# Ends of two-stream stages: row-scaled products behind the second root, low weight parts split behind the scaled columns, high-part products first

## The chip, the cores and the metric

One core of one Trainium2 chip runs the whole program in one launch. The metric is the device time of one execution in microseconds (us), as the median of several runs. TensorE (PE) does the matrix products, ScalarE (ACT) and VectorE (DVE) the work on columns and rows, GpSimd (POOL) some additions, SyncE (SP) issues the DMA transfers.

## The reference

A backbone of two layers over 512 tokens of width 1024: 256 context tokens (stream CS, columns 0 to 255 of every tile) and 256 latent tokens (stream XS, columns 256 to 511). Both streams use the same weights and differ in the modulation vectors. In each layer there are three sub-layers: a feed-forward net, a mixer (attention, mLSTM, HGRN2) and a second feed-forward net. All three have the same frame:

```
h = rms_norm(x, g_pre) * (1 + scale) + shift          # ada_pre
y = (silu(h @ w1) * (h @ w3)) @ w2                     # feed-forward; the mixer has its own
x = x + w * gate * rms_norm(y, g_post)                 # ada_post
```

So the end of one sub-layer and the start of the next hold two normalisations over the width in a row. The first needs the mean square of y, the second that of the new x; the new x depends on the first.

## The kernel before, in words

Activations lie transposed: 8 tiles of 128 channels (d = 0 to 7) by 512 tokens. `XT` is the residual x. A weight stage works on units of 512 rows by 256 columns: SP loads the unit as f32 into one of three `raw` buffers, ACT casts it to a high part `wh` (L238), DVE subtracts to get the low part `wl` (L239). There are four `wh` and four `wl` buffers. `h` is split in the same way into a high and a low half. Each product is then three matmuls (`mm3`): high by high (L255), high by low (L256), low by high (L257). A matmul has 256 tokens where the streams run one after the other, 512 where they run together.

**The stage end** (class `Post`). Each of the last output tiles y(d) is copied, squared and multiplied with XT by ACT and DVE, and column sums are taken on PE (L476, L478). They give, per stream, the mean squares of y, of the scaled y, of y times x and of x, and so both normalisations: a first reciprocal root y1 from the sum of y squared, then the mean square of the new x by a short formula, then a second root y2. Both are computed on DVE on 128 by 2 numbers (`rsqrt_cols`, L360 to L369). `steps` is a generator that is advanced from outside: it computes y1; yields; spreads y1 over the partitions on PE (`row_bcast`, L374) into the first half of a PSUM tile (`r`); computes y2; multiplies the eight y tiles by r on DVE (L530) and adds them to XT on POOL (L531); yields; spreads y2 into the second half of the same PSUM tile (`r2`, again L374, so it waits for the eight L530 that read the tile); yields; and forms h from XT and r2 by `scaled` (DVE, L389) and `split` (ACT for the high half, L397; DVE for the low half, L398).

**The stage start** (`passes`). Four accumulators (three PSUM banks `a`, one bank `b`) take a first pass over CS and a second one over XS, 8 channel tiles by 4 accumulators by 3 matmuls, 96 matmuls each. During the CS pass the steps of XS are pending, and `passes` advances them behind channel tiles 0, 2 and 5 and at its end. While the first four units of such a stage are loaded, `part_end` advances the steps of CS. There are four such stages with two streams: the mixers of both layers (mix0, mix1), the second feed-forward net of layer 0 (F1_0) and the first of layer 1 (F0_1). The last feed-forward net (F1_1) has only XS and also goes through `passes`; the very first one goes through its own path with a `hook`.

**What sets the order.** Each engine runs its instructions in the order in which the program holds them. A scheduler of the framework writes that order out when the program is built, from the order of the code, its own estimates of durations and readiness, and extra edges put in by `tc.issue_after(x)` (not before x in time). At a stage's end the units of the following columns (`wh`5 to `wh`8, as counted from the stage's first unit) are in that order too: their casts stand on ACT beside the splits of XS and the first reads of the finished accumulators. Those reads are, in a feed-forward net, silu (L611, one read of each of two accumulators) and in a mixer two activations (L839, L840, both read the same accumulator). PE's next products go to the banks that these reads set free.

Of the kernel before, what the change touches and what calls it, by code (L numbers as in the profile page):

```python
# [74 lines left out]
def body(tc, I, out, dbg=None):  # L75
    nc = tc.nc
    with tc.tile_pool(name="cst", bufs=1) as cst, \
# [9 lines left out]
        def nm(p):  # L87
            cnt[0] += 1
            return f"{p}{cnt[0]}"
# [153 lines left out]
        def unit(src, nk, hold=False, eng=None):  # L243
            res = []
            for b in range(0, nk, 4):
                n = min(4, nk - b)
                res += unit_split(unit_load(src[128 * b:128 * (b + n)], n), hold, eng)
            return res

        def mm3(ps, w, c0, h, a, b, first, last):  # L250
            n = len(w)
# [167 lines left out]
        class Post:  # L419
# [82 lines left out]
            def steps(self, st, pre, rest=None):  # L502


                if rest:
                    after = yield
                    with tc.issue_after(after):
                        rest()
                lo, hi, s = st
                y1 = rsqrt_cols(self.cs[s][:, :, 0], 2, 1.0 / D)  # L510
                t, m = small((128, 2, 4)), small((128, 2))
                V.tensor_scalar(t, self.cs[s], 1.0 / D, None, op0=ALU.mult)
                V.tensor_scalar(t[:, :, 2], t[:, :, 2], 2.0, None, op0=ALU.mult)
                V.tensor_scalar(t[:, :, 3], t[:, :, 3], EPS, None, op0=ALU.add)
                for i, q in ((2, t[:, :, 1]), (3, m)):
                    for k in range(2):
                        V.tensor_scalar(m[:, k:k + 1], q[:, k:k + 1], y1[:, k:k + 1], t[:, k, i:i + 1], op0=ALU.mult, op1=ALU.add)
                V.tensor_scalar(m, m, EPS, None, op0=ALU.max)
                after = yield
                rr = mx()  # L520
                r, r2 = rr[:, 0:256], rr[:, 256:512]
                with tc.issue_after(after) if after is not None else nullcontext():
                    row_bcast(y1, 0, 2, r)
                y2 = rsqrt_cols(None, 2, None, m)
                post_x.clear()
                for d in range(KD):
                    yt = self.y(d)[:, lo:hi]
                    xt = XT[:, d, lo:hi]
                    with tc.issue_after(tail[0]) if st is self.streams[-1] else nullcontext():
                        V.tensor_tensor(yt, yt, r, op=ALU.mult)  # L530
                    post_x.append(G.tensor_tensor(xt, xt, yt, op=ALU.add).ins)  # L531
                after = yield
                with tc.issue_after(after) if after is not None else nullcontext():
                    row_bcast(y2, 0, 2, r2)
                yield
                if pre.A is None:
                    pre.A = pre_cols(pre.l, pre.j, 0, KD)
                for d in range(KD):
                    pre.chunk(d, pre.A[:, d, :], st, r2)
                    if d % 4 == 3:  # L540
                        yield
# [44 lines left out]
        def passes(accs, h, sts, hook=None):  # L586
            settle()
            for p_ in pend[:-1]:
                while p_.left:
                    p_.step()  # L590
            for s_, (lo, hi, _) in enumerate(sts):
                for i in range(KD):
                    for j, (ps, w, c0) in enumerate(accs):
                        if hook:
                            hook(i, j)
                        end = mm3(ps[:, lo:hi], w[i:i + 1], c0, h[i:i + 1], lo, hi, i == 0, i == KD - 1)
                    if s_ == 0 and pend and (i, pend[-1].left) in ((0, 5), (2, 4), (5, 3)):
                        pend[-1].step(end)
                drain(end)

        def ffn(l, f, h, post, streams, pre, first=(None, None)):
# [16 lines left out]
            for gi in range(KF // 2):  # L618
                cols = slice(256 * gi, 256 * gi + 256)
                if gi == 0:  # L620
                    if units:
                        u1, u3 = units
                    else:
                        u1, u3 = [], []
                        for b0 in range(2):
                            with ExitStack() as es:
                                if len(streams) == 1:
                                    for e in (*post_done, *([post_x[2]] if b0 else [])):
                                        es.enter_context(tc.issue_after(e))
                                for u, w, e in ((u1, W1, G if b0 == 0 else V), (u3, W3, G if b0 == 0 else V)):  # L630
                                    u += unit(w[512 * b0:512 * b0 + 512, cols], 4, eng=e if len(streams) == 1 else V)
                            part_end()
                    ps = four()
                    passes([(ps[0], u1, 0), (ps[1], u1, 128), (ps[2], u3, 0), (ps[3], u3, 128)], h,
                           [(a, b, 0)] if hook else streams, hook)
# [188 lines left out]
        def mix(l, h, post, need_c, pre):  # L824
# [20 lines left out]

            us = [[], []]
            for b0 in range(2):
                for u in range(2):
                    us[u] += unit(Win[512 * b0:512 * b0 + 512, OFF_HF + 256 * u:OFF_HF + 256 * u + 256], 4)
                part_end()  # L850
            ps = four()
            passes([(ps[i], us[i // 2], 128 * (i % 2)) for i in range(4)], h, [CS, XS])
            for i in range(4):
# [595 lines left out]
```

## Time and profile before

| | us |
|---|---|
| median of 3 runs | 2438.77 |
| lowest, highest run | 2437.29, 3833.87 |
| the profiled execution | 2436.24 |
| span of its trace | 2434.4 |
| PE busy in the span | 2373.0 |
| ACT busy | 969.1 |
| DVE busy | 1477.4 |

PE is busy in 97% of the span, so the time is close to a sum of matmuls, and what can be won or lost at the same work is PE's idle time (the span less the busy time, 61 us, some of it at the start and the end) and the time in which the throttle granted half the clock. The view of windows gives the granted clock of a stretch as a share of the full one (PEclk); 0.50 is the lower of two levels, 1.2 GHz, and 1.00 the upper one, 2.4 GHz. The mean over the span is 0.985. The view of waits names, for each idle stretch of PE, the instruction that waited and the one that released it. In the timeline a row stands for one or several like instructions, with the start of the first and the time until the last one ended; a matmul of 256 columns is written with 0.28 us, but since matmuls overlap, they follow each other in less.

The stretches of the stages that the change touches, by the span's clock: mix0 405 to 460 us, F1_0 990 to 1065, F0_1 1405 to 1457, mix1 1800 to 1850, F1_1 2200 to 2250.

### The profile page before, as it was taken

To read this page: it belongs to the slowest core of one execution; us is meant where nothing else is said; L and a number is where in the kernel's file an instruction comes from. 1 tells how busy PE (TensorE), PEld (TensorE's weight loads), DVE (VectorE), ACT (ScalarE), POOL (GpSimd) and SP (SyncE) were. 2 spreads that over 40 slices of the span, in tenths; PEclk is the share of its full clock that TensorE was granted. 3 is DMA by queue.
4 is the path that set the end of the run, shared out by engine and by line. 5 is a ranking of instruction groups with operands and counts; after the bars stand their busy time and mean duration, and the time that the engine had idled before them with its cause. 6 is when DMAs were issued, how large, how long until landed. Compare 5 with 4: busy or idle time off the path is not lost.

```text
span 2434.4 us, 34696 instructions
## 1 busy us (share of the span) xinstructions
PE 2373.0 (97%) x13770; PEld 2008.1 (82%) x13770; DVE 1477.4 (61%) x2677; ACT 969.1 (40%) x1591; POOL 240.9 (10%) x233
## 2 busy tenths in 40 slices
PE   8999999999999999999999999999999989998998
PEld 5877878888787788887778888778799889797998
DVE  5687466655644643767946366874546657556554
ACT  3322332434643733432223332232334364754543
POOL 2000022100000112310002120001221000023000
PEclk9999999999999999999999999999999999998999
DMA  8655343311122032345543335653323115253664
GB/s 265 206 193 189 106 149 102 93 36 54 44 70 86 27 100 91 96 139 199 183 138 104 104 98 180 211 178 99 121 83 87 40 57 148 87 156 118 187 186 134
DMA packets 267270, 301.00 MB, mean 124 GB/s; under 512 B 11709, under 2 KB 233206, under 8 KB 267108
## 3 DMA queue, kind: packets, MB, share of 16 engines
q1 hardware_dynamic: 266448, 298.04, 39.2%
q8 instruction: 108, 1.77, 0.3%
q0 software_dynamic: 512, 0.68, 0.2%
q14 instruction: 54, 0.44, 0.1%
q10 hardware_dynamic: 148, 0.06, 0.0%
HBM read 297.70 MB, written 1.05 MB: 123 GB/s over the span
## 4 chain that ended last, share of the span: by engine, by line
PE 90%; DVE 5%; ACT 3%; issue 1%; DMA 1%; POOL 0%; SPq 0%; DVEq 0%; ACTq 0%; POOLq 0%
PE a L255 24%; PE a L256 24%; PE a L257 24%; PE a L767 1%; PE a L768 1%; PE a L769 1%; PE x L883 1%; PE x L320 1%; PE x L374 1%; PE b L1240 1%; PE x L1300 1%; PE x L1273 1%; PE b L256 1%; PE b L257 1%; PE b L255 1%
## 5 line engine op out<-in xcount | busy, mean ns | idle before, releaser
L255 PE MATMUL a<-s,wh 128*128 128x512 f32 (+1 forms) x3266 | 1144.8, 352 | 7.7 <-ACT s L397 7.2
L256 PE MATMUL a<-s,wh 128*128 128x512 f32 (+1 forms) x3266 | 1142.5, 350 | 3.2 <-DVE s L398 2.8
L257 PE MATMUL a<-s,wl 128*128 128x512 f32 (+1 forms) x3266 | 1141.1, 350 | 0.0
L239 DVE TENSOR_TENSOR wl<-raw,wh 128x1024 fp32r<-128x1024 f32 (+1 forms) x414 | 515.9, 1257 | 467.0 <-ACT wh L238 465.0
L255 PEld LDWEIGHTS a<-s,wh 128*128 128x128 f32 x3266 | 618.7, 190 | 110.0 <-ACT wh L238 10.1
L256 PEld LDWEIGHTS a<-s,wh 128*128 128x128 f32 x3266 | 620.5, 190 | 90.4 <-DVE s L398 4.9
L257 PEld LDWEIGHTS a<-s,wl 128*128 128x128 f32 x3266 | 620.1, 190 | 87.6 <-DVE s L615 2.5
L238 ACT CAST wh<-raw 128x1024 fp32r<-128x1024 f32 (+1 forms) x418 | 431.3, 1035 | 607.3 <-PE a L256 427.6
L311 DVE SCALAR_TENSOR_TENSOR s<-s,sc,s 128x512 f32<-128x512 f32 x448 | 306.7, 758 | 0.0
L415 POOL TENSOR_TENSOR s<-s,t 128x512 f32<-128x512 f32 (+1 forms) x35 | 52.4, 1496 | 1019.3 <-ACT s L411 1017.0
L612 DVE TENSOR_TENSOR u<-u,a 128x512 f32<-128x512 f32 (+1 forms) x84 | 51.8, 619 | 101.8 <-PE a L257 99.0
L614 ACT CAST s<-u 128x512 fp32r<-128x512 f32 (+1 forms) x88 | 49.0, 567 | 143.2 <-DVE u L612 125.5
L611 ACT ACTIVATE u<-a 128x512 f32<-128x512 f32 (+1 forms) x88 | 47.5, 542 | 144.8 <-PE a L257 144.8
L397 ACT ACTIVATE s<-t,mod 128x256 fp32r<-128x256 f32 x88 | 38.6, 500 | 93.7 <-DVE t L389 93.7
L767 PE MATMUL a<-wh,s 128*128 128x256 f32 x256 | 73.0, 285 | 2.1 <-ACT s L770 2.1
L768 PE MATMUL a<-wl,s 128*128 128x256 f32 x256 | 73.0, 285 | 0.3 <-DVE wl L239 0.3
L769 PE MATMUL a<-wh,s 128*128 128x256 f32 x256 | 72.8, 284 | 0.0
L531 POOL TENSOR_TENSOR XT<-XT,s 128x256 f32<-128x256 f32 x72 | 56.7, 826 | 132.7 <-DVE s L530 58.3
L1173 POOL TENSOR_TENSOR s<-s,u 128x512 f32<-128x512 f32 (+1 forms) x32 | 35.8, 1121 | 318.6 <-ACT wh L238 172.6
L615 DVE TENSOR_TENSOR s<-u,s 128x512 fp32r<-128x512 f32 (+1 forms) x88 | 53.4, 620 | 15.6 <-ACT s L614 15.2
L461 POOL TENSOR_TENSOR s<-s,u 128x512 f32<-128x512 f32 (+1 forms) x29 | 36.8, 1269 | 209.7 <-DVE u L457 200.4
L446 ACT ACTIVATE s<-a,R 128x256 f32<-128x256 f32 x77 | 34.1, 472 | 53.3 <-PE a L257 46.7
(345 smaller groups left out, 2373.8 us busy)
## 6 DMA issues: line engine op xcount, KB each, us to landing
raw<-in_ffn_w_dram SPq DMA_DIRECT2D x256, 512.0 KB, 3.8
s<-in_w_ada_dram SPq DMA_DIRECT2D x144, 512.0 KB, 6.0
raw<-in_w_in_dram SPq DMA_DIRECT2D x112, 512.0 KB, 3.7
raw<-in_w_out_dram SPq DMA_DIRECT2D x16, 512.0 KB, 3.5
raw<-in_ffn_w_dram SPq DMA_DIRECT2D x16, 256.0 KB, 2.6
raw<-in_w_branch_hg_dram SPq DMA_DIRECT2D x8, 512.0 KB, 4.1
raw<-in_w_branch_ml_dram SPq DMA_DIRECT2D x8, 512.0 KB, 3.3
raw<-in_w_branch_att_dram SPq DMA_DIRECT2D x8, 512.0 KB, 4.6
```

The source lines that it names most:

```text
L238: S.copy(hi[:, :n], raw[:, :n])
L239: (eng or V).tensor_tensor(lo[:, :n], raw[:, :n], hi[:, :n].bitcast(F32), op=ALU.subtract)
L255: mm(ps, hi, h[i][:, 0, a:b], start=first and i == 0, stop=False)
L256: mm(ps, hi, h[i][:, 1, a:b], start=False, stop=False)
L257: end = mm(ps, lo, h[i][:, 0, a:b], start=False, stop=last and i == n - 1)
L311: V.scalar_tensor_tensor(t[:, s], w, c, t[:, s], op0=ALU.mult, op1=ALU.add)
L415: eng.tensor_tensor(dst[:, a:b], dst[:, a:b], q[:, a:b], op=ALU.add)
L531: post_x.append(G.tensor_tensor(xt, xt, yt, op=ALU.add).ins)
L615: V.tensor_tensor(gt[:, 1, a:b], t[:, a:b], gt[:, 0, a:b].bitcast(F32), op=ALU.subtract)
L767: mm(ps, h[k][:, 0, tk], hi, start=k == 0, stop=False)
L768: mm(ps, h[k][:, 0, tk], lo, start=False, stop=False)
L769: mm(ps, h[k][:, 1, tk], hi, start=False, stop=k == KD - 1)
```

## The change

Three edits. (1) In `steps` the eight products y times r (L530) are held back behind the second root for both streams; before, only for the last stream. (2) A function `unit_parts` loads and casts a unit and hands the low subtraction back as a function; in the four two-stream stages the first units are cast at once and their low parts are subtracted after `part_end`, that is behind the scaled columns of CS. (3) `passes` works on blocks of four channel tiles: first all matmuls with the high weight part (both halves of h), then those with the low part. The pending steps of XS are advanced behind tiles 0 and 4 and at the end of the pass, so that y2 is spread only after the CS pass. The path with `hook` keeps its order. Behind line 249 the line numbers of the changed kernel are higher by 9, in `passes` and later by more.

```diff
+        def unit_parts(src, nk):
+            raw = raw_load(src, nk)
+            hi = stg.tile([128, 4, 256], F32R, name=nm("wh"), tag="wh", bufs=NHI)
+            lo = stg.tile([128, 4, 256], F32R, name=nm("wl"), tag="wl", bufs=NHI)
+            S.copy(hi[:, :nk], raw[:, :nk])
+            return [(hi[:, i], lo[:, i]) for i in range(nk)], lambda: V.tensor_tensor(
+                lo[:, :nk], raw[:, :nk], hi[:, :nk].bitcast(F32), op=ALU.subtract)
...
-                    with tc.issue_after(tail[0]) if st is self.streams[-1] else nullcontext():
+                    with tc.issue_after(tail[0]):
                         V.tensor_tensor(yt, yt, r, op=ALU.mult)
...
-                for i in range(KD):
-                    for j, (ps, w, c0) in enumerate(accs):
-                        if hook:
-                            hook(i, j)
-                        end = mm3(ps[:, lo:hi], w[i:i + 1], c0, h[i:i + 1], lo, hi, i == 0, i == KD - 1)
-                    if s_ == 0 and pend and (i, pend[-1].left) in ((0, 5), (2, 4), (5, 3)):
-                        pend[-1].step(end)
+                def one(ps, w, h_, part, i):
+                    for wi, hj in ((0, 0), (0, 1)) if part == 0 else ((1, 0),):
+                        e = mm(ps[:, lo:hi], w, h_[:, hj, lo:hi], start=i == 0 and part == 0 and hj == 0, stop=i == KD - 1 and part == 1)
+                    return e.ins
+                for i0 in range(0, KD, 1 if hook else 4):
+                    blk = range(i0, i0 + (1 if hook else 4))
...
+                    for part in range(2):
+                        for i in blk:
+                            for ps, w, c0 in accs:
+                                end = one(ps, w[i][part][:, c0:c0 + 128], h[i], part, i)
+                            if part == 0 and s_ == 0 and pend and (i, pend[-1].left) in ((0, 5), (4, 4)):
+                                pend[-1].step(end)
                 drain(end)
...
                         for b0 in range(2):
+                            if len(streams) == 2:
+                                los = []
+                                for u, w in ((u1, W1), (u3, W3)):
+                                    w, lo = unit_parts(w[512 * b0:512 * b0 + 512, cols], 4)
+                                    u += w
+                                    los.append(lo)
+                                part_end()
+                                for lo in los:
+                                    lo()
+                                continue
...
             us = [[], []]
             for b0 in range(2):
+                los = []
                 for u in range(2):
-                    us[u] += unit(Win[512 * b0:512 * b0 + 512, OFF_HF + 256 * u:OFF_HF + 256 * u + 256], 4)
+                    w, lo = unit_parts(Win[512 * b0:512 * b0 + 512, OFF_HF + 256 * u:OFF_HF + 256 * u + 256], 4)
+                    us[u] += w
+                    los.append(lo)
                 part_end()
+                for lo in los:
+                    lo()
```

The scheduler writes a new order from this. ScalarE at the end of the XS pass of mix0: before, from the third-last split of h to the reads of the first accumulators (`wh` names with 3763 to 3841 are the four units of the next columns, `a` the accumulators).

```order
L397 ACTIVATE s_3446<-t_3645,mod_88 128x256
L397 ACTIVATE s_3451<-t_3649,mod_88 128x256
L397 ACTIVATE s_3456<-t_3653,mod_88 128x256
L238 CAST wh_3763<-raw_3761 128x1024
L238 CAST wh_3769<-raw_3767 128x1024
L839 ACT_TABLE_LOAD
L839 ACTIVATE s_3376<-a_3459 128x512
L840 ACTIVATE s_3378<-a_3459 128x512
```

And the same place in the changed kernel:

```order
L406 ACTIVATE s_3444<-t_3645,mod_88 128x256
L238 CAST wh_3763<-raw_3761 128x1024
L406 ACTIVATE s_3449<-t_3649,mod_88 128x256
L406 ACTIVATE s_3454<-t_3653,mod_88 128x256
L238 CAST wh_3769<-raw_3767 128x1024
L238 CAST wh_3835<-raw_3833 128x1024
L238 CAST wh_3841<-raw_3839 128x1024
L870 ACT_TABLE_LOAD
L870 ACTIVATE s_3376<-a_3459 128x512
L871 ACTIVATE s_3378<-a_3459 128x512
```

The third and the fourth cast, which stood behind all eight reads, now stand ahead of the first. The other four stages show the same: two casts ahead of the reads before, four now; in F0_1 there is no table load between.

TensorE in the CS pass of F0_1, around the second half of XS's column sums (the rows that read `R`): before, these come behind 52 matmuls of the pass.

```order
L255 MATMUL a_11439<-s_11421,wh_11409 128x256
L256 MATMUL a_11439<-s_11421,wh_11409 128x256
L257 MATMUL a_11439<-s_11421,wl_11410 128x256
L255 MATMUL a_11440<-s_11421,wh_11409 128x256
L478 MATMUL x_11317<-R_10355,s_11365 128x1
L476 MATMUL x_11317<-R_10355,s_11365 128x2
L478 MATMUL x_11317<-R_10355,s_11365 128x1
L256 MATMUL a_11440<-s_11421,wh_11409 128x256
```

In the changed kernel they come behind 73.

```order
L604 MATMUL b_11442<-s_11429,wh_11414 128x256 x2
L604 MATMUL a_11439<-s_11434,wh_11409 128x256
L487 MATMUL x_11317<-R_10355,s_11365 128x1
L485 MATMUL x_11317<-R_10355,s_11365 128x2
L487 MATMUL x_11317<-R_10355,s_11365 128x1
L604 MATMUL a_11439<-s_11434,wh_11409 128x256
L604 MATMUL a_11440<-s_11434,wh_11409 128x256 x2
```

So 21 more matmuls stand ahead of the sums, and 23 instead of 44 behind them in the pass. mix1 has the same counts; in mix0 they are 61 before and 65 now.

## Rows read from the trace of the kernel before

**Rows 1.** The page's engine table: busy us, share of the span, instructions.

```profile
PE 2373.0 (97%) x13770; PEld 2008.1 (82%) x13770; DVE 1477.4 (61%) x2677; ACT 969.1 (40%) x1591; POOL 240.9 (10%) x233
```

**Rows 2.** Waits of PE in mix0, 405 to 465: total us, times, longest.

```profile
PE x L374 <- DVE s L530: 3.6, 2, 2.4
PE a L255 <- ACT s L397: 1.5, 2, 1.2
```

**Rows 3.** Waits of PE in F0_1, 1405 to 1465.

```profile
PE x L374 <- DVE s L530: 1.4, 1, 1.4
PE a L255 <- ACT s L397: 1.2, 1, 1.2
PE a L256 <- DVE s L398: 0.8, 2, 0.5
```

**Rows 4.** Waits of PE in mix1, 1795 to 1860.

```profile
PE x L374 <- DVE s L530: 1.3, 1, 1.3
```

**Rows 5.** Waits of PE in F1_0, 985 to 1070.

```profile
PE a L255 <- ACT s L397: 0.2, 1, 0.2
```

**Rows 6.** Timeline of PE in F0_1: start, us, engine, line, idle before and releaser.

```profile
1433.16 0.28 PE L478 MATMUL x<-R,s 128*128 128x1 f32 x2
...
1438.36 0.28 PE L257 MATMUL a<-s,wl 128*128 128x256 f32 x1
...
1439.42 0.28 PE L257 MATMUL b<-s,wl 128*128 128x256 f32 x1
1441.06 0.71 PE L374 MATMUL x<-cf,m 128*128 128x128 f32 x4 [1.36 <-DVE s L530]
1442.96 0.62 PE L255 MATMUL a<-s,wh 128*128 128x256 f32 x3 [1.19 <-ACT s L397]
...
1454.85 0.28 PE L257 MATMUL b<-s,wl 128*128 128x256 f32 x1
```

**Rows 7.** Timeline of DVE in F0_1, end of the second root and low parts.

```profile
1438.27 2.73 DVE L530 TENSOR_TENSOR s<-s,x 128x256 f32<-128x256 f32 x8
...
1449.82 2.36 DVE L239 TENSOR_TENSOR wl<-raw,wh 128x1024 fp32r<-128x1024 f32 x2 [0.45 <-ACT wh L238]
```

**Rows 8.** Timeline of ACT in F0_1, end of the XS pass.

```profile
1454.09 1.09 ACT L611 ACTIVATE u<-a 128x512 f32<-128x512 f32 x2 [3.35 <-PE a L257]
1455.07 1.05 ACT L238 CAST wh<-raw 128x1024 fp32r<-128x1024 f32 x1
```

**Rows 9.** Timeline of SP in F0_1: the loads of the next units.

```profile
1451.08 1.50 SPq L224 DMA_DIRECT2D raw<-in_ffn_w_dram  x2
```

**Rows 10.** The page's DMA issues: count, size, us from issue to landing.

```profile
raw<-in_ffn_w_dram SPq DMA_DIRECT2D x256, 512.0 KB, 3.8
s<-in_w_ada_dram SPq DMA_DIRECT2D x144, 512.0 KB, 6.0
```

**Rows 11.** Timeline of ACT in mix0, end of the XS pass.

```profile
453.06 1.28 ACT L839 ACT_TABLE_LOAD   x1
456.46 0.60 ACT L839 ACTIVATE s<-a 128x512 f32<-128x512 f32 x1 [2.12 <-PE a L257]
```

**Rows 12.** Windows: stretch, us, busy of PE, PEld, DVE, ACT, POOL, PEclk, DMA.

```profile
441.70:448.60 6.90, 5.71 (x27) 5.41 (x27) 6.04 (x14) 2.89 (x7) 3.15 (x5) 0.51 0.00 0
612.40:619.20 6.80, 6.80 (x21) 5.30 (x20) 3.90 (x6) 2.26 (x3) 0.00 (x0) 0.50 0.01 2
1436.00:1446.00 10.00, 7.21 (x57) 6.60 (x56) 8.91 (x33) 1.73 (x5) 5.71 (x8) 1.00 0.01 2
1834.40:1841.20 6.80, 6.34 (x29) 6.29 (x30) 6.62 (x15) 3.42 (x8) 1.98 (x3) 0.50 0.00 1
```

**Rows 13.** Waits of PE from 600 to 625.

```profile
PE x L1032 <- DVE s L1018: 3.2, 1, 3.2
```

**Rows 14.** Timeline of ACT at 85 to 89: a table load and the read behind it.

```profile
86.50 1.28 ACT L611 ACT_TABLE_LOAD   x1 [3.13 <-PE a L257]
87.80 0.60 ACT L611 ACTIVATE u<-a 128x512 f32<-128x512 f32 x1
```

More of the change, by code (lines that the diff above doesn't have):

```diff
@@ L591, in passes @@
             for s_, (lo, hi, _) in enumerate(sts):
-                for i in range(KD):
-                    for j, (ps, w, c0) in enumerate(accs):
-                        if hook:
-                            hook(i, j)
-                        end = mm3(ps[:, lo:hi], w[i:i + 1], c0, h[i:i + 1], lo, hi, i == 0, i == KD - 1)
-                    if s_ == 0 and pend and (i, pend[-1].left) in ((0, 5), (2, 4), (5, 3)):
-                        pend[-1].step(end)
+                def one(ps, w, h_, part, i):
[4 more added lines that the diff above has]
+                    blk = range(i0, i0 + (1 if hook else 4))
+                    if hook:
+                        for j, (ps, w, c0) in enumerate(accs):
+                            hook(i0, j)
+                            end = mm3(ps[:, lo:hi], w[i0:i0 + 1], c0, h[i0:i0 + 1], lo, hi, i0 == 0, i0 == KD - 1)
+                        continue
[5 more added lines that the diff above has]
+                                pend[-1].step(end)
                 drain(end)
@@ L625, in ffn @@
                         for b0 in range(2):
+                            if len(streams) == 2:
[7 more added lines that the diff above has]
+                                    lo()
+                                continue
                             with ExitStack() as es:
@@ L631, in ffn @@
                                     u += unit(w[512 * b0:512 * b0 + 512, cols], 4, eng=e if len(streams) == 1 else V)
-                            part_end()
                     ps = four()
```

## The prediction

> **What bounds the kernel now.** I read the page's engine table first: PE is busy 2373.0 us of a span of 2434.4 [rows 1]. The matmuls of the change are the same in number and size, so only PE's idle time and its clock can move. Then, for each stage that the diff touches, the waits of PE. The reader sees the same pair of idle stretches between the CS pass and the XS pass: the spread of y2 (L374) waits for the last product y times r (L530), 2.4 us in mix0, 1.4 in F0_1, 1.3 in mix1, and the first XS matmul waits for the first half of h, 1.2 each [rows 2 to 4]. In F1_0 only 0.2 is lost there [rows 5], since other work covers it. These rows add up to 3.6 + 1.5 + 1.4 + 1.2 + 0.8 + 1.3 + 0.2 = 10.0 us, the idle time at which the edits are directed. The timeline of F0_1 shows the chain: first column sum of XS 1433.16, last CS matmul 1439.42, spread of y2 1441.06, first XS matmul 1442.96 [rows 6]; on DVE the eight L530 take 2.73, to 1441.00 [rows 7]. So the spread comes 7.9 us behind the first column sum, and work on PE between the two is all that covers the chain. Last I read the windows for the clock. The 3.6 us of idle in mix0 were followed by 6.9 us at a granted clock of 0.51, the lower level, and mix1's pair by 6.8 us at 0.50; F0_1's pair, as long, was followed by no such stretch (1.00) [rows 12]. A wait of 3.2 us elsewhere [rows 13] was followed by 6.8 us at 0.50, PE busy throughout: 3.4 us lost.
>
> **The change, part by part.** A matmul of 256 columns costs (1439.42 - 1438.36) / 9 = 0.118 us [rows 6].
>
> *The start of the XS pass.* With high parts first, 21 more matmuls of F0_1's CS pass stand ahead of XS's last column sums: 21 x 0.118 = 2.5 us later. Against that, the waits of 0.8 for the low half of h mostly go, as does about 0.4 of refilling beside them. The sums come 1.3 later, and with them the spread, whose chain on DVE is unchanged: +1.3 (bounds +0.5, if the early waits shrink further, and +2.5, if none goes). The idle in front of the spread is then no longer 1.4 but the 7.9 less 0.6 for the sums, 23 matmuls (2.7) and the spread of y1 (0.4): 4.2 us. The same for mix1: +1.3. In mix0 only 4 more matmuls (0.5) stand ahead, and the first of the two L374 waits, 3.6 - 2.4 = 1.2, goes because CS's L530 no longer lie inside the first root; about 0.5 of that is given back waiting for the halves of h: -0.2 (bounds -1.2 and +0.5). In F1_0 y2 was spread ahead of the last 8 matmuls and is now spread behind them: 8 x 0.118 = 0.9. Further, a POOL addition on which an ACT copy ahead of CS's first split depends now stands behind all eight additions to XT, for about 0.9 more: +1.8 (bounds 0 and +2.5). Sum: **+4.2**, bounds -0.7 and +8.
>
> *The end of the XS pass.* This is the largest term, and it comes from ScalarE's order: four casts instead of two stand ahead of the reads that set the first accumulator free. The fourth cast needs its raw buffer filled. With three raw buffers its load is issued once the first low part of the new units is subtracted; before, those subtractions run at 1449.82, two in 2.36, so the first ends at 1451.0 [rows 7], and SP issues the loads at 1451.08 [rows 9]. The landing takes 3.8 [rows 10], to 1454.9, and the cast 1.05 [rows 8], to 1455.9. PE's pass ends at 1454.85 + 0.12 = 1455.0 [rows 6]. In the changed order the first cast stands two splits earlier but those two splits, and the subtraction behind them, as much later, so this chain keeps its length: the fourth cast ends about 1.0 behind the pass (bounds: 0, if the subtraction runs as soon as its buffer is free; 2.2 more if the load takes the 6.0 of the other kind of load [rows 10]). Before, it had nobody behind it but the next cast; now PE's next product waits for the reads behind it. Per stage: F0_1 1.0 + one read 0.6 (the two take 1.09 [rows 8]) = 1.6. F1_0 has a table load of 1.28 [rows 11] in between: 1.0 + 1.3 + 0.6 = 2.9. In mix0 and mix1 both reads are of the first accumulator: 1.0 + 1.3 + 1.1 = 3.4 each, less 0.1 that PE waits there now. F1_1, with reads half as wide (an estimate, 0.4): 2.7. Sum 1.6 + 2.9 + 3.3 + 3.3 + 2.7 = **+13.8**. Lower bound: were the casts done in time, the last matmul of the first accumulator would still stand 4th from the end of the pass rather than 10th, 6 x 0.118 = 0.7 later, which takes up the slack of the reads: at most 0.7 in mix0 and mix1, 0.5 in F1_0 and F0_1, 0.3 in F1_1, together +2.7.
>
> The two rows of a table load and the read behind it show the read starting 87.80 - 86.50 = 1.30 us behind the load's start [rows 14], so 1.3 is what the sum takes. The Trainium skill ("ScalarE: Activation LUTs", What ACT_TABLE_LOAD costs) puts a switch at 2.66 us, a load of 1283 ns and a drain of 1380 ns. By that page the four stages with a table load would cost 5.5 us more; the rows show the load's 1.28 and no drain behind it.
>
> *The clock.* In mix0 and mix1 the half-clock stretch is there already; a longer idle takes a little of it, -1. In F0_1 a wait of 4.2 + 1.2 is longer than any of the rows that a drop followed: a stretch like mix0's, 27 matmuls in 5.71 us of busy time, loses some 2.8 [rows 12]: net **+2** (bounds -1, +3). The new waits at the end of the XS passes are single ones of 3.3 in mix0 and mix1, next to the 3.2 [rows 13] that was followed by a drop: 2 x 3.4 = **+6.8**. Those of 2.9 and 2.7 lie between the 3.2 and the pair of 1.4 and 1.2 that had none; I take no drop, bounds 0 and 2 x 3.4.
>
> *At nothing.* The low subtractions behind the scaled columns are the same four on DVE; the low parts are first needed 32 matmuls (3.8 us) into the CS pass. If that cover failed, a subtraction of 1.2 [rows 7] would show. Two weight loads of SP in F1_0 and one in F0_1 move ahead of modulation loads, whose readers come over 15 us after their landing. POOL's additions are unchanged in number.
>
> Sum: 4.2 + 13.8 + 2 + 6.8 = 26.8. On the profiled execution, 2436.24 (its span is 2434.4, 1.8 lies around it): 2463.0. The runs shown have a median of 2438.77 and a lowest of 2437.29, so this execution is 1 to 2.5 us low; I forecast **2464**.
>
> **The rivals.** About 2% (49 us) is what a measurement of this kernel can tell from no change.
>
> *A, the forecast:* casts ahead of the reads cost 1.6 to 3.4 a stage, two new clock drops. Chance 0.50; its own range 2455 to 2476.
>
> *B, the casts are done in time.* The loads land sooner than the chain says, and the end of the pass costs 2.7 alone, with no drop: 4.2 + 2.7 + 2 = +8.9, 2445 to 2447. For it: the first cast is issued earlier, and the subtraction needs only 46 matmuls of the pass to be done, 50 x 0.118 = 5.9 before its end; 1.2 + 3.8 + 1.05 then just fit. Against it: the subtraction stands behind the last low half of h on DVE. Chance 0.22.
>
> *C, not slower.* High-first order and the free DVE let the halves of h come ahead of PE as intended: the 10.0 us of idle go, and with them the drops of mix0 and mix1 (2.8 + 3.2), less B's 2.7: -13.3, 2423 to 2426. It decides where XS's column sums start early enough for 7.9 us of PE work to lie behind them; the order has 23 matmuls there, 2.7 us, so the rows speak against it. Any mixture with B lies between 2426 and 2445. Chance 0.17.
>
> *D, every gap drops the clock and the loads are late.* The fourth cast's load takes the 6.0 us that its neighbours on the queue take, 5 x 2.2 = 11 more, and F1_0 and F1_1 drop too, 6.8: 2464 + 18 = 2482; with the upper bounds of the XS starts (+3.8) and of the clock in F0_1 and a third drop there, 2490. It decides from a landing over 5 us. Against it: 3.8 is the median of 256 such loads [rows 10]. Chance 0.11, half of it over 2%.
>
> The Trainium skill ("TensorE: Matmul & The Clock Gate", Architectural detail) says that ACT and DVE are strictly first in, first out: nothing behind the waiting cast can overtake it, whatever is ready. That is the premise of A against B's better half; ACT's rows here show each read where the order has it, and none that would contradict it.
>
> **How the numbers follow.** The likeliest case is A: 2464. The range is 2439 to 2478: it takes in A, B, the upper part of C's mixtures and the lower part of D. Faster by over 2% would need 49 us less, more than all idle time that the edits touch: 0.01. Slower by over 2%, above 2487: half of D, 0.05. Within 2%: 0.94.
>
> **What would show it.** In the changed profile, the waits of PE should name ACT's reads (now L870, L871, L633) at the end of five XS passes, with 1.5 to 3.4 us each, ACT's timeline four casts in a row ahead of them, and the cast before the table load waiting for DMA. The spread of y2 in F0_1 and mix1 should wait about 4 us for L539, the L530 of before. The windows should show 0.50 behind the ends of mix0 and mix1 and in F0_1's XS pass. I am wrong if the reads start at the pass's end, or if the XS sums are not later, or if PE's busy time rises elsewhere.

## The result, and the profile after

The changed kernel takes 2456.7 us (median of 4 runs, 2453.57 to 2459.03) against 2438.03 for the kernel before in the same comparison, so 18.7 us slower by the medians. One of before's four runs was a slow one (3833.87); the ratio leaves it out and is 1.0085, 95% interval 1.0074 to 1.0097, which is some 20.7 us. The forecast was 2464, range 2439 to 2478. The profiled execution of the changed kernel, 2459.03, is the slowest of its four; its span of 2457.2 is 22.8 longer than the profiled one of before. So the single stretches below belong to that pair of executions and add up to more than the medians differ.

The waits of PE in the five stages, in the changed kernel, in the order mix0 (405 to 465), F1_0 (985 to 1080), F0_1 (1405 to 1480), mix1 (1795 to 1880), F1_1 (2195 to 2290), answer to [rows 2 to 5]. L264 is the L255 of before behind the passes, L604 the matmuls inside them, L383 the spread.

```profile
PE a L264 <- ACT s L871: 2.9, 1, 2.9
PE x L383 <- DVE s L539: 2.6, 1, 2.6
...
PE a L264 <- ACT u L633: 2.4, 1, 2.4
PE b L604 <- ACT s L406: 1.4, 2, 0.9
...
PE x L383 <- DVE s L539: 3.6, 1, 3.6
PE a L604 <- ACT s L406: 1.2, 1, 1.2
PE a L264 <- ACT u L633: 1.1, 1, 1.1
...
PE x L383 <- DVE s L539: 3.6, 1, 3.6
PE a L264 <- ACT s L871: 3.0, 1, 3.0
...
PE a L264 <- ACT u L633: 2.2, 1, 2.2
```

The reader is to see two things. The first is a row that before did not have: PE's next product (L264) waits for ScalarE's read of the first accumulator, behind every one of the five XS passes, 2.9 + 2.4 + 1.1 + 3.0 + 2.2 = 11.6 us (before, such a wait was at most 0.11). The second is that the spread of y2 in F0_1 and mix1 now waits 3.6 where it waited 1.4 and 1.3 [rows 3, 4], while the first of mix0's two spreads no longer waits (one wait of 2.6 for two, 3.6 together [rows 2]).

ScalarE at the end of mix0's XS pass, the place of [rows 11]; under it SP's loads and DVE's low parts at the same place.

```profile
452.53 1.04 ACT L238 CAST wh<-raw 128x1024 fp32r<-128x1024 f32 x1
456.46 1.05 ACT L238 CAST wh<-raw 128x1024 fp32r<-128x1024 f32 x1 [2.89 <-issue]
458.11 1.05 ACT L238 CAST wh<-raw 128x1024 fp32r<-128x1024 f32 x1 [0.60 <-DMA raw<-in_w_in_dram]
459.17 1.28 ACT L870 ACT_TABLE_LOAD   x1
460.46 0.60 ACT L870 ACTIVATE s<-a 128x512 f32<-128x512 f32 x1
```

```profile
454.35 7.01 SPq L224 DMA_DIRECT2D raw<-in_w_in_dram  x4
```

```profile
453.06 2.35 DVE L239 TENSOR_TENSOR wl<-raw,wh 128x1024 fp32r<-128x1024 f32 x2
```

The low part of the first new unit is done at 454.2 (the first half of the row at 453.06), SP issues the load at 454.35, the fourth cast waits for that load until 458.11, and only then come the table load and the reads. PE had finished its pass at 458.75, and its next product starts at 461.60.

The clock, answering to [rows 12]: a stretch in F1_0's CS pass, the end of F1_0, F0_1's and mix1's XS starts, the ends of mix1 and mix0.

```profile
1036.90:1043.70 6.80, 6.20 (x28) 5.82 (x28) 5.29 (x12) 3.06 (x7) 2.38 (x3) 0.51 0.00 0
...
1072.00:1078.00 6.00, 4.19 (x11) 3.32 (x12) 4.26 (x6) 3.46 (x5) 0.00 (x0) 0.72 0.68 184
...
1453.00:1460.00 7.00, 4.45 (x18) 3.95 (x19) 5.61 (x14) 2.24 (x6) 4.57 (x7) 0.53 0.00 0
...
1849.00:1856.00 7.00, 4.58 (x18) 4.10 (x19) 5.60 (x15) 2.38 (x6) 4.43 (x7) 0.53 0.00 0
1870.00:1874.00 4.00, 4.00 (x24) 4.00 (x23) 3.48 (x7) 2.21 (x5) 1.95 (x2) 0.59 0.56 182
...
460.00:470.00 10.00, 8.40 (x36) 6.81 (x37) 6.16 (x12) 5.08 (x10) 1.29 (x1) 1.00 0.35 105
```

F0_1 has the half-clock stretch that it did not have before, and F1_0 has two, in its CS pass and behind its end; behind mix0's end, 2.9 us of wait, there is none. PE's busy time over the span rose with the time at the lower clock:

```profile
PE 2381.3 (97%) x13770; PEld 2016.1 (82%) x13770; DVE 1475.4 (60%) x2677; ACT 971.3 (40%) x1591; POOL 241.6 (10%) x233
```

The same matmuls took 2381.3 against 2373.0 [rows 1], 8.3 more. PE's idle time (the span less the busy time) rose from 61.4 to 75.9, 14.5 more. The two make up the 22.8.

### The profile page after: what moved, and what is told of

Read it like the earlier page. It is cut to its first block, busy times and chain, and to the rows that moved or that the text cites. A ratio compares the mean times of both kernels' runs of the same rounds, so it can differ in the third digit from the quotient of the medians.

```text
span 2457.2 us, 34692 instructions
## 1 busy us (share of the span) xinstructions
PE 2381.3 (97%) x13770; PEld 2016.1 (82%) x13770; DVE 1475.4 (60%) x2677; ACT 971.3 (40%) x1591; POOL 241.6 (10%) x233
## 4 chain that ended last, share of the span: by engine, by line
PE 89%; DVE 5%; ACT 3%; DMA 1%; issue 1%; POOL 1%; SPq 0%; DVEq 0%; ACTq 0%; POOLq 0%
PE a L264 23%; PE a L266 23%; PE a L265 23%; PE a L604 2%; PE a L798 1%; PE a L799 1%; PE a L800 1%; PE x L383 1%; PE x L919 1%; PE x L329 1%; PE b L1276 1%; PE x L1336 1%; PE b L604 1%; PE x L1309 1%; DMA raw<-in_ffn_w_dram 1%
## 5 line engine op out<-in xcount | busy, mean ns | idle before, releaser
L264 PE MATMUL a<-s,wh 128*128 128x512 f32 (+1 forms) x3050 | 1084.5, 356 | 15.4 <-ACT s L871 5.8
L265 PE MATMUL a<-s,wh 128*128 128x512 f32 (+1 forms) x3050 | 1079.4, 354 | 0.6 <-DVE s L805 0.3
L266 PE MATMUL a<-s,wl 128*128 128x512 f32 (+1 forms) x3050 | 1078.9, 354 | 0.0
L239 DVE TENSOR_TENSOR wl<-raw,wh 128x1024 fp32r<-128x1024 f32 (+1 forms) x398 | 491.9, 1246 | 479.4 <-ACT wh L238 461.0
L264 PEld LDWEIGHTS a<-s,wh 128*128 128x128 f32 x3050 | 578.2, 190 | 116.0 <-ACT wh L238 10.1
L238 ACT CAST wh<-raw 128x1024 fp32r<-128x1024 f32 (+1 forms) x402 | 415.0, 1033 | 610.7 <-PE a L265 431.1
L266 PEld LDWEIGHTS a<-s,wl 128*128 128x128 f32 x3050 | 578.0, 190 | 87.5 <-DVE s L637 2.5
L265 PEld LDWEIGHTS a<-s,wh 128*128 128x128 f32 x3050 | 578.4, 190 | 86.7 <-issue 3.7
L604 PE MATMUL a<-s,wh 128*128 128x256 f32 x432 | 73.8, 307 | 6.7 <-ACT s L406 6.0
L604 PEld LDWEIGHTS a<-s,wh 128*128 128x128 f32 x432 | 63.3, 208 | 9.2 <-ACT s L406 7.3
L1209 POOL TENSOR_TENSOR s<-s,u 128x512 f32<-128x512 f32 (+1 forms) x32 | 35.8, 1120 | 317.2 <-ACT wh L238 171.2
```

The source lines that it names most:

```text
L238: S.copy(hi[:, :n], raw[:, :n])
L239: (eng or V).tensor_tensor(lo[:, :n], raw[:, :n], hi[:, :n].bitcast(F32), op=ALU.subtract)
L264: mm(ps, hi, h[i][:, 0, a:b], start=first and i == 0, stop=False)
L265: mm(ps, hi, h[i][:, 1, a:b], start=False, stop=False)
L266: end = mm(ps, lo, h[i][:, 0, a:b], start=False, stop=last and i == n - 1)
L604: e = mm(ps[:, lo:hi], w, h_[:, hj, lo:hi], start=i == 0 and part == 0 and hj == 0, stop=i == KD - 1 and part == 1)
```

## The experiments

A measured time is the median in us. Ratios are to the kernel before, run beside each on the same chip, with the 95% interval. Stretches of a trace belong to the one profiled execution of each kernel.

**e1: edit (3) alone**, against the kernel before.

```diff
-                for i in range(KD):
-                    for j, (ps, w, c0) in enumerate(accs):
...
-                        end = mm3(ps[:, lo:hi], w[i:i + 1], c0, h[i:i + 1], lo, hi, i == 0, i == KD - 1)
+                for i0 in range(0, KD, 1 if hook else 4):
...
+                    for part in range(2):
+                        for i in blk:
```

> The kernel before with edit (3) alone: products in blocks of four, high parts first, in both passes. Theory (ScalarE's order is the main cost, and it comes from the high-first XS pass): PE waits for the first reads of the accumulators behind all five XS passes, 1.1 to 3.0 us each, 11.5 together as in the changed kernel; the XS column sums stay behind 52 matmuls, so the spread of y2 waits 1.3 to 1.4 as before; +0.9 in F1_0 where y2 is now spread at the pass's end; clock drops behind some ends, some 3 us. 2450 to 2456. Rival (the casts move ahead because the deferred low parts free DVE and the raw buffers differently, the main cost is the late column sums): no waits at the ends, 2438 to 2441.

Measured 2452.92, 1.0061 (1.0046 to 1.0075). Waits of PE in e1, F0_1 and then mix1; L595 are the matmuls of the passes:

```profile
PE x L374 <- DVE s L530: 1.4, 1, 1.4
PE a L595 <- ACT s L397: 1.2, 1, 1.2
PE a L255 <- ACT u L624: 1.0, 1, 1.0
...
PE a L255 <- ACT s L853: 2.9, 1, 2.9
PE x L374 <- DVE s L530: 1.3, 1, 1.3
```

The spread waits as before; the reads hold PE as in the changed kernel. All five ends show it: 2.8, 2.5, 1.0, 2.9, 2.3, together 11.5. ACT's timeline has four casts ahead of the reads in all five. So the high-first order brings the four casts ahead of the reads, and this is the largest part of the loss. Why the scheduler does it no run shows. A reading that fits: with high parts first, the last matmul that reads a high part stands 16 places from the end of the pass, so the third and fourth `wh` buffer come free before the pass ends, and in the changed kernel the third cast starts at 456.46, in the middle of mix0's last high-part matmuls.

**e2: edits (1) and (2) alone**, against the changed kernel: the passes of before.

```diff
-                for i0 in range(0, KD, 1 if hook else 4):
...
+                for i in range(KD):
+                    for j, (ps, w, c0) in enumerate(accs):
...
+                        end = mm3(ps[:, lo:hi], w[i:i + 1], c0, h[i:i + 1], lo, hi, i == 0, i == KD - 1)
```

> The changed kernel with edit (3) undone: edits (1) and (2) alone. Theory: two casts ahead of the reads again, so no wait of more than 0.2 at the ends of the XS passes; the column sums of XS in F0_1 and mix1 stay behind 73 matmuls, so the spread of y2 waits about 3.6 there with a half-clock stretch in F0_1, and F1_0 keeps its early drop: 2442 to 2448. Rival (the deferred low parts are what puts casts ahead): waits at the ends remain, 2453 to 2457.

Measured 2444.45, 1.0022 (1.0013 to 1.0031). Waits of PE in F0_1 in e2:

```profile
PE x L383 <- DVE s L539: 3.6, 1, 3.6
PE a L264 <- ACT s L406: 1.2, 1, 1.2
```

No wait of over 0.11 at the five ends, the whole lateness of the sums in F0_1 and mix1. For these two the theory held. Its third part did not: in F1_0 the wait of 0.9 for h is not there (the longest is 0.4), nor the drop right behind it. In this execution PE ran at half clock earlier, from 1012 to 1022, ahead of the same late additions of POOL, and again for 3.4 us from 1045.9.

**e3: edit (1) alone**, against the kernel before.

```diff
-                    with tc.issue_after(tail[0]) if st is self.streams[-1] else nullcontext():
+                    with tc.issue_after(tail[0]):
```

> The kernel before with edit (1) alone: y times r behind the second root for both streams. Theory: in mix0 the 1.2 us wait of the first spread goes, but in F1_0 the additions to XT on POOL start behind the second root, some 7 us later, so the first halves of h of CS come late, PE waits about 0.7 more there and the clock drops for 6.8 us as in the changed kernel (3.4 us lost): net +2 to +4, 2440 to 2442. Rival (the early drop in F1_0 of the changed kernel is due to the order of the products or to the deferred low parts, not to this edit): -1 to 0, 2437.

Measured 2436.24, 0.9994 (0.9986 to 1.0003): no difference that can be told, and so not the 2 to 4 us of my theory. Its mechanism is there, its price is not. In F1_0 POOL's additions to XT start behind the second root, and PE waits for the first half of h (first row: waits of PE in e3, 985 to 1080; second: timeline of POOL in e3, where before had all eight in one row; third: a window of e3, with the granted clock 0.76):

```profile
PE b L255 <- ACT s L397: 1.3, 2, 0.9
```

```profile
1018.44 2.13 POOL L531 TENSOR_TENSOR XT<-XT,s 128x256 f32<-128x256 f32 x3 [1.81 <-DVE s L530]
```

```profile
1037.00:1044.00 7.00, 7.00 (x49) 7.00 (x49) 4.75 (x31) 0.00 (x0) 0.44 (x1) 0.76 0.00 0
```

That stretch at 0.76 loses half as much as the one in the changed kernel, but it starts 9 us behind the last of these waits, and e1, without edit (1) and without the wait of 0.9, has one of the same length at 1042.6. So edit (1) is not shown to be its cause. In mix0 one of the two waits of the spread has gone:

```profile
PE x L374 <- DVE s L530: 2.9, 1, 2.9
```

That this gain pays for F1_0 is a reading; what is shown is that edit (1) alone is neutral.

**e4: high parts first in the CS pass alone**, in `passes` of the changed kernel.

```diff
+                    if s_ == len(sts) - 1:
+                        for i in blk:
+                            for ps, w, c0 in accs:
+                                end = mm3(ps[:, lo:hi], w[i:i + 1], c0, h[i:i + 1], lo, hi, i == 0, i == KD - 1)
+                        continue
```

> The changed kernel with high parts first in the CS pass alone; the XS pass (and the single pass of F1_1) runs in the order of before. Theory: the high-first order of the pass that ends at the reads is what lets the casts of the third and fourth unit go ahead: here two casts stand ahead, no wait at the ends, and the drops behind them go too: 11.5 us of waits and 3 to 5 of clock less than the changed kernel, 2440 to 2444. Rival (the time at the ends is lost in another way, the raw loads or the low parts being late for the next product): the waits go to the next product, 2450 to 2456.

Measured 2442.74, 1.0022 (1.0014 to 1.0031), the same as e2. The waits at the ends are gone. So of edit (3) it is the order in the pass that ends at the reads which costs, and its use in the CS pass brings nothing measurable.

**e5: the changed kernel with the third and fourth cast held behind the first reads.** In `unit_split`, `held[0]` is for these two casts the last read of the first accumulator in a mixer, the second silu in a feed-forward net.

```diff
-                S.copy(hi[:, :n], raw[:, :n])
+                with tc.issue_after(held[0]) if held[0] is not None else nullcontext():
+                    S.copy(hi[:, :n], raw[:, :n])
```

> The changed kernel with one thing more: the casts of the third and fourth unit of the next columns are held behind the first accumulator's reads, so that two casts stand ahead of the reads, as before, while both passes keep the high-first order. Theory (ScalarE's in-order casts cause the waits at the ends): the five waits of 11.5 us shrink to 0 to 0.8 each, what is left is the first accumulator's last matmul standing 4th from the end: 2440 to 2446. Rival (the high-first order itself costs it, all four accumulators being finished only in the last four matmuls): waits of over 1 us remain in mix0 and mix1, over 2448.

Measured 2443.86, 1.0037 (1.0025 to 1.0049). Waits of PE in mix0 in e5 (L267: the product behind the pass):

```profile
PE x L386 <- DVE s L542: 2.6, 1, 2.6
...
PE a L267 <- ACT s L883: 0.8, 1, 0.8
```

The five ends wait 0.8, 0.3, 0.3, 0.8 and under 0.1, where they waited 11.6. This is the most direct test: in its trace PE's 13770 matmuls come in the order of the changed kernel, and only the place of two casts on ScalarE differs (two stand ahead of the reads in all five stages). Of the 0.85% that the change costs 0.48 are back, some 12 us. The short half-clock stretches behind the ends of F1_0 and mix1 are not there in this execution either. The rest at the ends is what the sum had as its lower bound, the last matmul of the first accumulator standing 4th from the end.

**e6: a buffer of its own for the fourth unit's raw weights**, in `unit` of the changed kernel.

```diff
+                if own[0] and b == 4:
+                    res += unit_split([(raw_load(src[128 * b:128 * (b + n)], n, slab(shape=(128, 4, 256))), n)], hold, eng)
+                    continue
```

> The changed kernel with a buffer of its own (from the slab pool) for the raw weights of the fourth unit of the next columns. In the order this gives, three casts stand ahead of the first reads and the fourth, with its load, behind them. Theory (the one cast whose load can only be issued behind a low part of the new units is what holds the reads; a cast that has its data costs nothing there): no wait over 0.8 at the five ends, 2440 to 2446. Rival (the time of the casts themselves on ScalarE holds the reads, each 1.05): waits of 1 to 2 us remain, 2446 to 2452.

Measured 2445.19, 1.0043 (1.0031 to 1.0055). The time is inside the theory's range, the waits are between theory and rival. Waits of PE in mix0 in e6:

```profile
PE x L388 <- DVE s L544: 2.6, 1, 2.6
PE a L269 <- ACT s L880: 1.2, 1, 1.2
```

1.2 in mix0 and mix1, 0.7, 0.3 and 0.4 in the others. Without the fourth cast's late load ahead of the reads, 7.8 of the 11.6 go; some is left in the mixers with the third cast and the table load ahead of them, and F1_1 has a new wait of 0.6 for a low part. As the scheduler put the fourth cast behind the reads here, e6 does not separate the buffer from the order; e5's statement is the firmer one.

**e7: late low parts.** In `passes` of e4's kernel, behind channel tile 0 of the CS pass; `rest_cols` writes CS's second half of columns and then the second pair of low parts.

```diff
+                            if part == 0 and s_ == 0 and i == 0 and los:
+                                rest_cols()
```

> The variant of e4 (high parts first in the CS pass alone), with the low parts of the second pair of units and the second half of the scaled columns of CS written behind the last products of XS in the program, so that DVE reaches the product of XS's last tile with XT earlier: in the order the column sums of XS stand behind 26 matmuls of the CS pass in F0_1 and mix1 and behind 17 in mix0, not 73 and 65. Theory (the sums are late because that product stands last in DVE's queue, behind low parts and columns): the spread of y2 waits under 0.5 in all three stages, the drops of the clock there are rarer, F1_0 keeps its 1.6 more: 2423 to 2433. Rival (DVE's chain gets as much longer, through columns and low parts interleaved with it, as it starts earlier, or PE waits for them): 2434 to 2442.

Measured 2434.07, 0.9993 (0.9984 to 1.0001): the upper edge of the theory's range missed by 1, the rival's lower edge met. That is 7 to 9 less than e4 (by the ratios, by the medians). Waits of PE in F0_1 in e7, and DVE between the two roots there:

```profile
PE x L383 <- DVE s L539: 2.3, 1, 2.3
```

```profile
1427.95 0.16 DVE L369 TENSOR_SCALAR m<-x 128x2 f32<-128x2 f32 x1 [1.12 <-PE x L487]
...
1431.29 1.22 DVE L256 TENSOR_TENSOR wl<-raw,wh 128x1024 fp32r<-128x1024 f32 x1
1432.42 0.45 DVE L526 TENSOR_SCALAR m<-m,m 128x1 f32<-128x1 f32 x2
...
1433.62 1.22 DVE L256 TENSOR_TENSOR wl<-raw,wh 128x1024 fp32r<-128x1024 f32 x1
...
1436.26 2.73 DVE L539 TENSOR_TENSOR s<-s,x 128x256 f32<-128x256 f32 x8
```

The sums do come early, as the theory says. For comparison, the start of the same chain in the kernel before:

```profile
1433.92 0.16 DVE L360 TENSOR_SCALAR m<-x 128x2 f32<-128x2 f32 x1 [0.90 <-PE x L478]
```

But the chain from there to the eight L539 takes 1436.26 - 1427.95 = 8.3 us where before, with DVE free for it, the same two instructions started at 1433.92 and 1438.27 [rows 7], 4.35 apart. The two low parts and four columns went from ahead of the chain into it.

**e8: e7, with edit (1) not for the mixers' ends.**

```diff
-                    with tc.issue_after(tail[0]):
+                    with tc.issue_after(tail[0]) if st is self.streams[-1] or self.mk[1] != 1 else nullcontext():
```

> As e7, but edit (1) not for the post stage of the mixers, so that in F1_0 the additions to XT start behind the first root again. Theory: the wait of 0.9 ahead of F1_0's CS pass shrinks to 0.2 and a clock drop there is rarer: 0.7 to 4 less than e7, 2420 to 2431. Rival (F1_0's drop is not due to that wait): as e7.

Measured 2431.42, 0.9988 (0.9977 to 0.9998): the fastest version of all, ahead of the kernel before by an interval that barely excludes no change. The wait of 0.9 in F1_0 is gone (0.13 is left of it). Against e7 the time is 2.7 less by the medians, inside what was expected, but the two intervals overlap and the means differ by 1.3 only, so a gain of e8 over e7 is not shown.

**e9: e8, with the late low parts on POOL.** In `unit_parts`, with `eng` POOL for the second pair of units.

```diff
-            return [(hi[:, i], lo[:, i]) for i in range(nk)], lambda: V.tensor_tensor(
+            return [(hi[:, i], lo[:, i]) for i in range(nk)], lambda: (eng or V).tensor_tensor(
```

> As e8, but the low parts of the second pair of units are subtracted on POOL instead of DVE. In e7 the two subtractions of 1.2 stood inside XS's chain on DVE, between the first and the second root. Theory (what is left of the wait of the spread, 2.2 in F0_1 and mix1 and 1.2 in mix0, is those 2.4 us and nothing else): the spread waits 0 to 0.4 in all three, 5 us of idle less than e8 and less clock loss: 2421 to 2428. Rival (POOL's subtraction, 2.4 each in the trace of before, and DVE slowed beside it make the chain or the low parts late: PE then waits for wl in the second block of the CS pass): 2429 to 2435.

Measured 2446.64, 1.0044 (1.0032 to 1.0057): the rival, and worse than its range. POOL and then DVE in F0_1 in e9:

```profile
1431.31 5.68 POOL L256 TENSOR_TENSOR wl<-raw,wh 128x1024 fp32r<-128x1024 f32 x2
```

```profile
1431.46 3.33 DVE L256 TENSOR_TENSOR wl<-raw,wh 128x1024 fp32r<-128x1024 f32 x1
1434.71 2.95 DVE L407 SCALAR_TENSOR_TENSOR s<-t,mod,s 128x256 fp32r<-128x256 f32 x2
1437.59 0.41 DVE L477 TENSOR_TENSOR s<-b,XT 128x256 f32<-128x256 f32 x1
```

While POOL subtracts, a DVE subtraction takes 3.33 instead of 1.2 and two split halves 2.95 instead of 0.9. The product L477, which the move was to bring forward, comes some 4 us later by that (2.1 + 2.1), and PE waits 3.3 us for h in the CS pass of F0_1 and of mix1. The first half of the theory came true: the spread of y2 no longer waits in F0_1, mix1 or mix0. The time went to the other place.

**e10: edit (2) alone**, against the kernel before, here the mixers' lines.

```diff
-                    us[u] += unit(Win[512 * b0:512 * b0 + 512, OFF_HF + 256 * u:OFF_HF + 256 * u + 256], 4)
+                    w, lo = unit_parts(Win[512 * b0:512 * b0 + 512, OFF_HF + 256 * u:OFF_HF + 256 * u + 256], 4)
...
                 part_end()
+                for lo in los:
+                    lo()
```

> The kernel before with edit (2) alone: low parts of the first units behind the scaled columns of CS. In the order XS's column sums stand behind 71 matmuls in F0_1 and mix1 and behind 73 in mix0. Theory (edit 2 is the source of the late sums, and so of what e2 costs over e3): the spread of y2 waits 3.3 to 3.7 in F0_1 and mix1 and over 3 in mix0, no wait at the ends of the XS passes: 2440 to 2446. Rival (the late sums come only from edits 1 and 2 together): 2436 to 2438.

Measured 2439.60, 1.0018 (1.0008 to 1.0027), 0.4 below the theory's range and above the rival's. The lateness is there without edit (1) and without edit (3); the first row is mix0, the second F0_1:

```profile
PE x L383 <- DVE s L539: 4.8, 2, 3.6
...
PE x L383 <- DVE s L539: 3.4, 1, 3.4
```

In ratio, edit (1) -0.06%, edit (2) +0.18%, edit (3) +0.61% add up to +0.73%; all three together have +0.85% with an interval of 0.74 to 0.97.

## Why the prediction was right, point by point

**ScalarE's order.** The forecast's mechanism and its largest term. Forecast 13.8, seen 11.6 of new waits less the 0.2 that were there: 11.4. The size was off because the fourth cast ends 459.16 - 458.75 = 0.4 behind the pass in mix0, not 1.0: the first low part is done 4.2 before the last matmul starts (454.24 to 458.47), where the sum had 3.85 (1451.0 to 1454.85), and the profile ends that matmul 0.28 behind its start, where the sum took 0.12. The landing, the table load of 1.28 and the reads are as in the sum. So 0.3 to 0.5 a stage is missing, in each of the five. That the place of the casts, and not something else in the high-first order, holds PE is shown by e5; that the casts came ahead through edit (3), by e1 and e2.

**The late sums.** Forecast a wait of 4.2 ahead of the spread, seen 3.6. The idle ahead of the XS pass rose by 1.4 in F0_1 (3.6 + 1.2 against 1.4 + 1.2 + 0.8) and by 1.6 in mix1, forecast 1.3 each; in mix0 it fell by 0.6, forecast 0.2. I ascribed the move to the high-first order ("with high parts first, 21 more matmuls stand ahead"). That step was wrong, and that the size came out near is luck as far as this cause goes: e1 has the high-first order and the spread waits as before, e10 has the low parts deferred and the sums late. The 21 matmuls were there, but it was edit (2) that put them there: the product of XS's last tile with XT comes last on DVE, behind the low parts, and the scheduler places the sums by it; e7, which moves it ahead, has the sums early.

**F1_0.** Forecast +1.8 ahead of its XS pass, of which 0.9 for y2's spread at the pass's end: the wait for h there went from 0.2 [rows 5] to 1.2, as it does in e1. The other 0.9, POOL's additions, is the 0.9 of the row above; e3 shows it with edit (1) alone, and e8 takes it away. In e2 and e5, which have edit (1) too, it is not seen; in both PE ran at half clock shortly ahead (from 1012 and from 1016). With the shorter waits of before set against it, the rise is 1.4 in all.

**The clock.** This term failed in its places, and that its size came near in the profiled pair (8.3 more busy time, forecast 8.8) is luck. F0_1's stretch came as forecast. Of the two drops forecast behind the ends of mix0 and mix1, mix0's did not come and mix1's stretch is short (0.59 over 4 us). F1_0 has two that the forecast had not: the early one, and one behind its end (0.72 over 6 us), where the forecast took none. The forecast took the rows of one execution as if a wait of a certain length always had the same result, which the runs do not bear out. In F1_0, e7 has the same waits of 0.9, 0.1 and 0.6 as the changed kernel, and the clock stays at its upper level (waits of PE in e7, 985 to 1080; a window of e7 around them); e6 is the same.

```profile
PE b L611 <- ACT s L406: 1.4, 2, 0.9
```

```profile
1024.00:1044.00 20.00, 18.19 (x145) 16.51 (x144) 13.84 (x48) 6.87 (x17) 6.51 (x9) 1.00 0.00 1
```

Nor do drops stand behind pairs of waits, as the forecast read them: in the kernel before, mix0's starts at 441.7, between the wait of 2.4 (to 441.45) and that of 1.2 (from 442.44), and in the changed kernel F0_1's starts at 1453.5, inside the wait of 3.6 (1450.75 to 1454.36).

**The sum.** 26.8 forecast; 18.7 by the medians, 20.7 by the ratio, 22.8 in the profiled pair. In that pair the ends have 11.4 for 13.8, the starts of the XS passes 3.8 for 4.2 (1.4 + 1.6 - 0.6 + 1.4), the clock 8.3 for 8.8, and 0.7 less idle lies elsewhere. That the medians differ by less fits the clock: of the four runs of the changed kernel the profiled one has the lowest mean clock, 0.980, and the fastest, 2453.57, has 0.984. How much of each term another run has, a single profile cannot say. Such a difference, 0.85%, stands well clear of no change here; the 2% that the forecast gave as the limit of what can be told was too coarse.

The forecast's 10.0 us of idle leaves out mix1's waits for the halves of h, 1.2 and 0.5, though its text counts the 1.2; the view of before has it below the row of [rows 4]:

```profile
PE a L255 <- ACT s L397: 1.2, 1, 1.2
```

Rival C's price rests on that sum, the forecast does not.

**The rivals.** B, that the casts would be done in time, fell with the profile: the fourth load lands about where the chain put it. C, that the idle would go, fell for the reason given, and e7 shows that its point of decision was the right one but that DVE, not PE's order, is then the bound. D did not happen as a whole: loads of 3.8 as before; of its further drops the one behind F1_0's end came, 3.4 us long.

The table load's row is followed by the read 1.29 us behind its start (459.17 to 460.46), as in [rows 14]. The Trainium skill ("ScalarE: Activation LUTs", What ACT_TABLE_LOAD costs) has a further 1380 ns for a drain; the trace does not agree: the cast ahead of the load ends at 459.16 and the read behind it starts at 460.46, so no drain stands on either side, and the measured 1.29 decides here.

What stays open: why a given wait is followed by a half-clock stretch in one run or kernel and not in another, how the clock's share of the 18.7 divides among the stages in other runs than the profiled one, and why the scheduler brings the casts ahead.

## What to carry to other kernels

A reordering of matmuls that leaves PE's work the same can still move what another engine's queue holds ahead of the work that PE waits for next: read the new order of ScalarE and VectorE at the place where accumulators are released, and follow the first instruction there that needs a transfer back to what lets that transfer start. When work is deferred out of a critical chain's way, look at what it is deferred into: here low parts put behind one stream's columns stood ahead of the next stream's last product, and put behind that product they stood inside its chain. Hold loads' consumers behind the reads that free a bank; here that change of place alone took back more than half of the loss.

## What was not expected of the hardware

DVE slows beside POOL more than the trace of before shows, where the longest subtraction of this kind takes 2.57 (at 36.12, beside one of POOL's): in e9, with two POOL subtractions of 128 by 1024 under way (5.68 together), it takes 3.33 against 1.21 alone; beside POOL's additions to XT, in the changed kernel at 1432.56, it takes 1.73. And the granted clock fell to 0.51 in F1_0 of the changed kernel at 1037.0, behind waits of 0.9 and 0.1 us and as a third of 0.6 began, while the same three waits in e7 and a single wait of 2.9 at mix0's end left it at 1.00.
